# Dense products with u in three float32r terms, u split one key ahead, at the end of a hybrid-trunk step

## The chip, the cores and the metric

The kernel runs on one core of one Trainium2 chip. The metric is the device time of one execution in microseconds. Times from the trace are counted from the start of the span of one profiled execution. TensorE appears as PE (matmuls) and PEld (weight loads), VectorE as DVE, ScalarE as ACT, GpSimd as POOL, SyncE as SP.

## What is computed

One layer of a streaming encoder over 1152 tokens: 1024 of a prompt and 128 of eight sample streams, nine tiles of 128 tokens with 1024 features. A mixer (a gating unit and a retention branch, merged and projected) is followed by a retrieval over 16384 single-neuron experts, and a final norm. The change is in the retrieval. Cut to what matters there:

```python
def _peer_block(t, w_query, k1, k2, eu, ev):
    q = (t @ w_query).reshape(T, P_HEADS, P_DKEY)
    s1 = jnp.einsum('thd,nd->thn', q[..., :P_HALF], k1)
    s2 = jnp.einsum('thd,nd->thn', q[..., P_HALF:], k2)
    v1, i1 = lax.top_k(s1, P_TOPK)
    v2, i2 = lax.top_k(s2, P_TOPK)
    ...                       # the 16 best pairs of each of 8 heads
    experts = e1 * P_NKEYS + e2
    w = jax.nn.softmax(vals, axis=-1)
    a = jax.nn.gelu(jnp.einsum('td,thkd->thk', t, eu[experts]))
    return jnp.einsum('thk,thkd->td', w * a, ev[experts])
```

A token has 128 experts (8 heads of 16). Each has a row u and a row v of 1024 float32 features. The token's product with u goes through a gelu, is weighed, and scales v, which is summed.

## The kernel before

The trunk works through three groups of tiles (0 and 1; 2 to 5; 6 to 8). Its weights come through a stream of units of 128x1024 float32, in the order of the list `order`. In the first two groups each unit is split into two float32r parts, and a product is made of three terms (high with high, low with high, high with low: `products`). In the third group, from `PLAIN` on, units are used as plain float32, and the buffers of the parts (`wraw`, `whi`, `wlo`, three each) all serve as unit buffers, nine in number. `room` says when a buffer of this ring may be loaded again: when the unit in it has been taken.

The retrieval is done in two ways. Tiles 0, 1, 2, 6, 7 and 8 are gathered: for each of a token's 128 experts GpSimd issues an indirect DMA that fetches u and v side by side for 128 tokens, a row buffer of 128x2048 float32 (line 865). VectorE makes the dot with the token (`dot`, line 818, two records: the product and a read of its accumulator), ScalarE the gelu and the weight (`weigh`, 823 and 824), VectorE adds the scaled v to the sum (`add`, 828). 768 such row buffers are worked off, one after the other. The ring of buffers is a list: five called `gat`; two called `st` once the dense tiles are expanded; and one called `gax`, added just ahead of the dense loop. `AHEAD` is how many gathers stand ahead of their dots in program order.

Tiles 3, 4 and 5 are dense: a table of the weights of all 128 x 128 experts is written to DRAM (`pdr`), and the dense loop (line 1030 on) goes over 128 keys, 128 experts each. For key e, TensorE multiplies u (eight blocks of 128x128, stationary) with the transposed tokens `tT` (384 columns) into a PSUM tile S (line 1040); ScalarE makes the gelu g (1042); VectorE multiplies g with the table's part pt (1044); and two keys later (`LEAD`) TensorE adds six products of g with v into six PSUM tiles `res` (1053). S has two buffers, g four, pt one per eight keys. `turn_dense` makes `tT` during the third group's queries.

The order of instructions on each engine is set when the program is built: the loops issue keys at high priority (`DP`) and rows at a pace (`PACE`, in us of an estimated clock that `advance` moves), and the scheduler orders all by what it estimates to be ready. Each engine then follows its own order. A row's dot that waits for its landing holds back everything behind it on VectorE.

Of the kernel before, what the change touches and what calls it, by code (L numbers as in the profile page):

```python
# [8 lines left out]
F32 = mybir.dt.float32  # L9
F32R = mybir.dt.float32r  # L10
# [7 lines left out]
P = 128  # L18
# [38 lines left out]
def step_kernel(ctx: ExitStack, tc: tile.TileContext, x, state, wall, wst, bs, rows, vec, cst, smp, cosd, sind, euv,  # L57
# [51 lines left out]

    for e in range(NKEYS + LEAD):  # L110
        order += [("u", e)] * (e < NKEYS) + [("v", e - LEAD)] * (e >= LEAD)
    NRAW, NPART, NBK = 3, 3, 2
# [23 lines left out]

    def room(n, now):
        ring = rings[homes[n % 3]]
        return ring[-NPART] < now

# [143 lines left out]
    def turn_dense(pl):  # L284

        tT = hTs["dense"] = pair_tiles(act, TD, "h", gi=PLAIN)
        for n, t in enumerate(DENSE):
            xt = pl.tile([P, D], F32, name="dx", bufs=2)
            nc.sync.dma_start(xt, tsp[t])
            yield  # L290
            for j in range(2):
                ps = sp.tile([P, 4, P], F32, name="sps")
                for k in range(4):
                    tr(ps[:, k], xt[:, (4 * j + k) * P:(4 * j + k + 1) * P], ident)
                split([w[:, 4 * j:4 * j + 4, n * P:(n + 1) * P] for w in tT], ps)
# [709 lines left out]

    tT, = hTs.pop("dense")
    while len(expanded) < len(DENSE):
# [5 lines left out]
    dg = ctx.enter_context(tc.tile_pool(name="dg", bufs=1))  # L1013
    gx = ctx.enter_context(tc.tile_pool(name="gx", bufs=1))
    dp = dense_sb.enter_context(tc.tile_pool(name="dp", bufs=1))
    dps = ctx.enter_context(tc.tile_pool(name="dps", bufs=1, space=bass.MemoryType.PSUM))
    rings_.append((gx, "gax", 1))
    AHEAD[0] += 1

# [4 lines left out]
    res = {o: dps.tile([P, 512], F32, name=f"res{o[0]}{o[1]}") for o in outs}  # L1024
    G = {}

    PACE[0] = 3.55
    for e in range(NKEYS + LEAD):
        if e < NKEYS:
            with tc.high_priority(DP):  # L1030
# [4 lines left out]
                ps = Ss.pop(e) if e in Ss else dps.tile([P, TD], F32, name="S", bufs=2)  # L1035
                u, (w,) = take()
                assert u == ("u", e)
                w = w.rearrange("p a b -> p (a b)")
                for k in range(KD):
                    mm(ps, w[:, k * P:(k + 1) * P], tT[:, k], start=k == 0, stop=k == KD - 1)  # L1040
                a = G[e] = dg.tile([P, TD], F32, name="g", bufs=4)
                nc.scalar.activation(a, ps, AF.Gelu_apprx_tanh)  # L1042
# [108 lines left out]
```

## Time and profile before

| | us |
|---|---|
| median of three runs | 3848.13 |
| lowest, highest | 3837.57, 3850.18 |
| the profiled execution | 3852.71 |
| its span | 3850.9 |
| TensorE busy in the span | 3569.9 (93%) |
| VectorE busy | 3088.8 (80%) |
| ScalarE busy | 1359.1 (35%) |
| GpSimd busy | 1097.9 (29%) |

The shares are means over the trunk and the dense loop. The dense loop starts at about 2390 us. What limits each part of it is read from the stretches, where the copies of the lists of expert rows (`idx`, line 802) for tiles 7 and 8 serve as marks that both programs have.

### The profile page before, as it was taken

The numbers are of one execution on the slowest core, as the hardware profiler recorded it, in microseconds if no ns is written. First come the engines' busy times: TensorE is split into PE (matmuls) and PEld (weight loads), VectorE is DVE, ScalarE is ACT, GpSimd is POOL, SyncE is SP. The second block draws the span as 40 slices with busy tenths as digits, with TensorE's granted clock in tenths as the row PEclk, the third lists the DMA queues.
The fourth block names the chain that finished last, engine by engine and source line by source line (L and its number), as shares of the span: only waits on it lengthen the run. The fifth ranks groups of instructions, "written<-read, shape, count | busy, mean of one in ns | idle before, by whom it ended". The sixth has DMA issues, their size and how long they took to land.

```text
span 3850.9 us, 45654 instructions
## 1 busy us (share of the span) xinstructions
PE 3569.9 (93%) x15681; PEld 2468.7 (64%) x15681; DVE 3088.8 (80%) x5859; ACT 1359.1 (35%) x3289; POOL 1097.9 (29%) x788
## 2 busy tenths in 40 slices
PE   8999999999989888989999989988999899999998
PEld 6789987877878776767667565544444454444444
DVE  5666699999989789999993679979877877777773
ACT  4455634444343532846545222211112111211111
POOL 0000002433434231132320332334433534443330
PEclk9999999999999999999999989999999999999999
DMA  8675547998989895799994998899999999999993
GB/s 313 238 259 189 195 152 285 363 352 328 359 321 375 340 372 214 246 344 316 365 346 146 369 410 338 337 411 374 418 419 418 419 418 419 419 418 419 418 419 153
DMA packets 300822, 1291.28 MB, mean 335 GB/s; under 512 B 28336, under 2 KB 92592, under 8 KB 200240
## 3 DMA queue, kind: packets, MB, share of 16 engines
q0 software_dynamic: 114944, 822.13, 53.6%
q1 hardware_dynamic: 185648, 466.25, 32.9%
q8 instruction: 124, 2.03, 0.2%
q14 instruction: 106, 0.87, 0.1%
HBM read 1221.16 MB, written 67.11 MB: 335 GB/s over the span
## 4 chain that ended last, share of the span: by engine, by line
DMA 26%; issue 22%; DVE 19%; PE 19%; POOL 11%; ACT 2%; SPq 0%; POOLq 0%; DVEq 0%; ACTq 0%
DMA gat<-in_euv_dram,idx 12%; POOL gat L865 9%; PE gps L210 9%; DMA st<-in_euv_dram,idx 8%; DVE acc L828 5%; PE gps L226 4%; DVE gat L818 3%; PE res L1053 2%; PE S L1040 2%; DMA s<-ssp 1%; DMA gax<-in_euv_dram,idx 1%; POOL st L865 1%; DVE ktmp L710 1%; DVE wlo L240 1%; DVE oh L794 1%
## 5 line engine op out<-in xcount | busy, mean ns | idle before, releaser
L865 POOL DMA_INDIRECT gat<-in_euv_dram,idx x600 | 848.3, 1414 | 1905.0 <-DVE acc L828 1158.3
L828 DVE SCALAR_TENSOR_TENSOR acc<-gat,sdot,acc 128x1024 f32<-128x1024 f32 x600 | 767.0, 1278 | 106.8 <-ACT sdot L824 103.3
L818 DVE CUSTOM_DVE_ANT_0 gat<-gat,tx 128x1024 f32<-128x1024 f32 x600 | 730.1, 1218 | 134.9 <-DMA gat<-in_euv_dram,idx 117.4
L823 ACT ACTIVATE sdot<-sdot 128x1 f32<-128x1 f32 x768 | 154.9, 203 | 1788.3 <-DVE sdot L818 1787.0
L226 PE MATMUL gps<-whi,h 128*128 128x256 f32 x2688 | 519.2, 301 | 6.9 <-ACT h L236 5.7
L226 PEld LDWEIGHTS gps<-whi,h 128*128 128x128 f32 x2688 | 437.7, 193 | 28.2 <-issue 10.1
L226 PE MATMUL gps<-wlo,h 128*128 128x256 f32 x1536 | 419.6, 312 | 8.8 <-issue 5.5
L210 PE MATMUL gps<-h,whi 128*128 128x256 f32 (+2 forms) x1520 | 407.4, 366 | 4.6 <-ACT th L591 3.2
L210 PE MATMUL gps<-y,whi 128*128 128x256 f32 (+2 forms) x1168 | 310.7, 362 | 9.4 <-DVE pb L382 4.8
L226 PEld LDWEIGHTS gps<-wlo,h 128*128 128x128 f32 x1536 | 295.9, 194 | 26.9 <-issue 13.0
L210 PEld LDWEIGHTS gps<-h,whi 128*128 128x128 f32 x1520 | 270.7, 193 | 62.3 <-ACT th L591 3.8
L210 PE MATMUL gps<-h,wlo 128*128 128x256 f32 (+2 forms) x864 | 292.8, 378 | 6.6 <-DVE wlo L240 6.4
L1040 PE MATMUL S<-h,wlo 128*128 128x384 f32 x672 | 252.3, 509 | 41.6 <-ACT g L1042 41.6
L1040 PE MATMUL S<-h,wraw 128*128 128x384 f32 x688 | 258.6, 510 | 29.0 <-ACT g L1042 28.4
L865 POOL DMA_INDIRECT st<-in_euv_dram,idx x118 | 164.7, 1396 | 370.5 <-DVE acc L828 229.4
L1040 PE MATMUL S<-h,whi 128*128 128x384 f32 x688 | 248.7, 493 | 21.7 <-ACT g L1042 21.6
L1053 PE MATMUL res<-wraw,g 128*128 128x512 f32 x516 | 243.1, 594 | 1.7 <-DVE g L1044 1.7
L1053 PE MATMUL res<-wlo,g 128*128 128x512 f32 x516 | 243.7, 592 | 0.5 <-DVE g L1044 0.5
L1040 PEld LDWEIGHTS S<-h,wlo 128*128 128x128 f32 x672 | 132.7, 200 | 170.0 <-issue 65.0
L1053 PE MATMUL res<-whi,g 128*128 128x512 f32 x504 | 240.1, 595 | 0.9 <-DVE g L1044 0.9
L210 PEld LDWEIGHTS gps<-y,whi 128*128 128x128 f32 x1168 | 206.4, 192 | 51.9 <-issue 7.4
L1040 PEld LDWEIGHTS S<-h,wraw 128*128 128x128 f32 x688 | 135.8, 199 | 158.5 <-issue 67.6
(230 smaller groups left out, 5686.7 us busy)
## 6 DMA issues: line engine op xcount, KB each, us to landing
wraw<-in_wall_dram SPq DMA_DIRECT2D x214, 512.0 KB
gat<-in_wall_dram SPq DMA_DIRECT2D x84, 512.0 KB
pdr<-st SPq DMA_DIRECT2D x24, 1024.0 KB
pt<-pdr SPq DMA_DIRECT2D x16, 1536.0 KB
wlo<-in_wall_dram SPq DMA_DIRECT2D x43, 512.0 KB
whi<-in_wall_dram SPq DMA_DIRECT2D x43, 512.0 KB
wraw<-in_eud_dram SPq DMA_DIRECT2D x43, 512.0 KB
whi<-in_eud_dram SPq DMA_DIRECT2D x43, 512.0 KB
```

The costliest lines, as they stand in the source:

```text
L210: mm(ps[:, c, :T], x, y, start=kh == 0 and k == 0 and j == 0, stop=kh == nk - 1 and k == 3 and j == len(pr) - 1)
L226: mm(ps[:, i], y, x, start=kh == 0 and k == 0 and j == 0 and i % 2 == 0, stop=kh == 1 and k == 3 and j == len(pr) - 1 and last)
L240: nc.vector.tensor_tensor(parts[1], src, parts[0].bitcast(F32), op=OP.subtract)
L710: nc.vector.match_replace(tmp, v[:, :8], src, -3.0e38)
L794: tt(oh, ij[:, c, hs, None].to_broadcast([P, n, TOPK]), iota[:, None, :].to_broadcast([P, n, TOPK]), op=OP.is_equal)
L818: nc.vector.tensor_tensor_reduce(out=b[:, :D], in0=b[:, :D], in1=d["x"], op0=OP.mult, op1=OP.add, scale=1.0, scalar=0.0, accum_out=d["s"][ ...
L823: nc.scalar.activation(d["s"][:, j:j + 1], d["s"][:, j:j + 1], AF.Gelu_apprx_tanh)
L828: nc.vector.scalar_tensor_tensor(d["acc"], b[:, D:], d["s"][:, j:j + 1], d["acc"], op0=OP.mult, op1=OP.add)
L865: nc.gpsimd.indirect_dma_start(out=b, out_offset=None, in_=euv, in_offset=bass.IndirectOffsetOnAxis(ap=d["idx"][:, j:j + 1], axis=0))
L1040: mm(ps, w[:, k * P:(k + 1) * P], tT[:, k], start=k == 0, stop=k == KD - 1)
L1053: mm(res[n, j], g[:, n * P:(n + 1) * P], w[:, 512 * j:512 * j + 512], start=e == LEAD, stop=e == NKEYS + LEAD - 1)
```

## The change

The dense products with u become three-term products. `turn_dense` makes `tT` in two float32r parts. A new function `halves` takes the next u and splits it: ScalarE copies it into `uhi` (float32r), VectorE subtracts to get `ulo`; both have two buffers. It is called once ahead of key 0, and then at key e for key e+1, behind the products of key e. A key's eight float32 products become 24 of float32r. So that u can be taken one key earlier, the list `order` puts v one place later, and `room` counts a unit of u as released at once by the split. The row buffer `gax` goes, and `AHEAD` stays one lower; g has three buffers instead of four.

```diff
-    for e in range(NKEYS + LEAD):
-        order += [("u", e)] * (e < NKEYS) + [("v", e - LEAD)] * (e >= LEAD)
+    for e in range(NKEYS + LEAD + 1):
+        order += [("u", e)] * (e < NKEYS) + [("v", e - LEAD - 1)] * (e > LEAD)
...
     def room(n, now):
         ring = rings[homes[n % 3]]
-        return ring[-NPART] < now
+        return ring[-NPART] < now - (type(order[ring[-NPART]]) is tuple and order[ring[-NPART]][0] == "u")
...
-        tT = hTs["dense"] = pair_tiles(act, TD, "h", gi=PLAIN)
+        tT = hTs["dense"] = pair_tiles(act, TD, "h")
...
-    gx = ctx.enter_context(tc.tile_pool(name="gx", bufs=1))
...
-    rings_.append((gx, "gax", 1))
-    AHEAD[0] += 1
...
+    us = []
+    def halves():
+        u, (w,) = take()
+        assert u[0] == "u"
+        w = w.rearrange("p a b -> p (a b)")
+        hi = dg.tile([P, D], F32R, name="uhi", bufs=2)
+        nc.scalar.copy(hi, w)
+        lo = dg.tile([P, D], F32R, name="ulo", bufs=2)
+        nc.vector.tensor_tensor(lo, w, hi.bitcast(F32), op=OP.subtract)
+        us.append((hi, lo))
...
-                u, (w,) = take()
-                assert u == ("u", e)
-                w = w.rearrange("p a b -> p (a b)")
+                if not e:
+                    halves()
+                w = us.pop(0)
                 for k in range(KD):
-                    mm(ps, w[:, k * P:(k + 1) * P], tT[:, k], start=k == 0, stop=k == KD - 1)
-                a = G[e] = dg.tile([P, TD], F32, name="g", bufs=4)
+                    pr = products([t[:, k * P:(k + 1) * P] for t in w], [t[:, k] for t in tT])
+                    for j, (x, y) in enumerate(pr):
+                        mm(ps, x, y, start=k == 0 and j == 0, stop=k == KD - 1 and j == 2)
+                if e + 1 < NKEYS:
+                    halves()
+                a = G[e] = dg.tile([P, TD], F32, name="g", bufs=3)
```

The scheduler orders the whole end anew. In the rows below, line 818 before is 820 after (dot), 828 is 830 (add), 1044 is 1059 (product with pt), 1040 is 1053 (product with u), 1053 is 1068 (product with v), 1067 is 1082 (a dense tile's sum), and 1035 is the new subtraction.

VectorE in the long stretch, before, from one key's product with pt to the next:

```order
L1044 TENSOR_TENSOR g<-g,pt 128x384
L828 SCALAR_TENSOR_TENSOR acc<-st,sdot,acc 128x1024
L818 ISA st,sdot<-st,tx 128x1024
L818 ISA sdot 128x1
L828 SCALAR_TENSOR_TENSOR acc<-st,sdot,acc 128x1024
L818 ISA gax,sdot<-gax,tx 128x1024
L818 ISA sdot 128x1
L828 SCALAR_TENSOR_TENSOR acc<-gax,sdot,acc 128x1024
L818 ISA gat,sdot<-gat,tx 128x1024
L818 ISA sdot 128x1
L1044 TENSOR_TENSOR g<-g,pt 128x384
```

The same place after:

```order
L1059 TENSOR_TENSOR g<-g,pt 128x384
L1035 TENSOR_TENSOR ulo<-whi,uhi 128x1024
L820 ISA gat,sdot<-gat,tx 128x1024
L820 ISA sdot 128x1
L830 SCALAR_TENSOR_TENSOR acc<-gat,sdot,acc 128x1024 x2
L820 ISA st,sdot<-st,tx 128x1024
L820 ISA sdot 128x1
L830 SCALAR_TENSOR_TENSOR acc<-st,sdot,acc 128x1024
L820 ISA st,sdot<-st,tx 128x1024
L820 ISA sdot 128x1
L1059 TENSOR_TENSOR g<-g,pt 128x384
```

The subtraction for the key two ahead stands behind the product with pt, and the dot ahead of that product has its add four instructions later instead of at once.

TensorE in the long stretch, before (S is the product with u, res the six sums with v; the numbers are buffers):

```order
L1040 MATMUL S_20831<-h0_18720,whi_20670 128x384 x5
L1053 MATMUL res00_19458<-wlo_20695,g_20762 128x512
L1040 MATMUL S_20831<-h0_18720,whi_20670 128x384
L1053 MATMUL res10_19459<-wlo_20695,g_20762 128x512
L1040 MATMUL S_20831<-h0_18720,whi_20670 128x384
L1053 MATMUL res20_19460<-wlo_20695,g_20762 128x512
L1040 MATMUL S_20831<-h0_18720,whi_20670 128x384
L1053 MATMUL res01_19461<-wlo_20695,g_20762 128x512
```

TensorE after:

```order
L1053 MATMUL S_22455<-h0_18720,uhi_22424 128x384
L1053 MATMUL S_22395<-h0_18720,uhi_22364 128x384
L1053 MATMUL S_22455<-h0_18720,ulo_22426 128x384
L1053 MATMUL S_22395<-h0_18720,ulo_22366 128x384
L1053 MATMUL S_22455<-h1_18721,uhi_22424 128x384
L1053 MATMUL S_22395<-h1_18721,uhi_22364 128x384
L1053 MATMUL S_22455<-h0_18720,uhi_22424 128x384
L1053 MATMUL S_22395<-h0_18720,uhi_22364 128x384
L1053 MATMUL S_22455<-h0_18720,ulo_22426 128x384
L1053 MATMUL S_22395<-h0_18720,ulo_22366 128x384
L1068 MATMUL res00_19462<-whi_22300,g_22368 128x512
L1053 MATMUL S_22455<-h1_18721,uhi_22424 128x384
```

The products of one key are now often mixed with those of the next, and with single float32 products with v.

VectorE at the end, before: the last row's dot and add, the last six keys' products with pt, and the dense tiles' sums.

```order
L818 ISA gat,sdot<-gat,tx 128x1024
L818 ISA sdot 128x1
L828 SCALAR_TENSOR_TENSOR acc<-gat,sdot,acc 128x1024
L1044 TENSOR_TENSOR g<-g,pt 128x384 x6
L1067 TENSOR_TENSOR dx<-dx,res_19458 128x512
L1067 TENSOR_TENSOR dx<-dx,res_19459 128x512
```

VectorE after, around the last key's product with pt:

```order
L1059 TENSOR_TENSOR g<-g,pt 128x384
L830 SCALAR_TENSOR_TENSOR acc<-st,sdot,acc 128x1024
L820 ISA st,sdot<-st,tx 128x1024
L820 ISA sdot 128x1
L830 SCALAR_TENSOR_TENSOR acc<-st,sdot,acc 128x1024
L1082 TENSOR_TENSOR dx<-dx,res_19462 128x512
L1082 TENSOR_TENSOR dx<-dx,res_19465 128x512
L820 ISA gat,sdot<-gat,tx 128x1024
L820 ISA sdot 128x1
```

Behind the last key's product there are now 24 dots and 25 adds of rows, and the dense sums stand among them.

## Rows read from the trace of the kernel before

**Rows 1.** The page's 40 slices: busy share of DMA in tenths, and GB/s.

```profile
DMA  8675547998989895799994998899999999999993
GB/s 313 238 259 189 195 152 285 363 352 328 359 321 375 340 372 214 246 344 316 365 346 146 369 410 338 337 411 374 418 419 418 419 418 419 419 418 419 418 419 153
```

**Rows 2.** Stretches: length; PE, PEld, DVE, ACT, POOL busy (x); clock, DMA share, GB/s.

```profile
2434.00:2486.00 52.00, 52.00 (x143) 26.87 (x142) 50.29 (x138) 13.63 (x33) 20.59 (x16) 1.00 1.00 397
2486.00:2897.00 411.00, 373.26 (x977) 188.55 (x975) 341.26 (x620) 70.83 (x268) 175.24 (x118) 0.96 1.00 406
2897.00:3785.00 888.00, 830.84 (x2182) 421.94 (x2182) 674.36 (x858) 168.20 (x607) 337.76 (x250) 0.97 1.01 414
...
3768.00:3851.00 83.00, 70.28 (x187) 35.04 (x185) 26.88 (x37) 12.74 (x32) 0.00 (x0) 0.95 0.30 110
```

**Rows 3.** Timeline of DVE: start, duration; the lists for tiles 7 and 8.

```profile
2485.91 0.22 DVE L802 CAST idx<-m 128x128 int32<-128x128 f32 x1
...
2896.85 0.22 DVE L802 CAST idx<-m 128x128 int32<-128x128 f32 x1
```

**Rows 4.** The chain that ended last, in the dense loop: start, duration, what.

```profile
3746.00 4.51 PE S L1040 x14
3750.51 4.29 PE res L1053 x10
3756.31 4.51 PE S L1040 x14
```

**Rows 5.** Timeline of PE in the trunk: three-term products, 512 and 256 columns.

```profile
302.12 0.28 PE L210 MATMUL gps<-y,wlo 128*128 128x256 f32 x1
...
302.46 0.28 PE L210 MATMUL gps<-y,wlo 128*128 128x256 f32 x1
...
700.35 0.39 PE L210 MATMUL gps<-y,wlo 128*128 128x512 f32 x1
...
701.04 0.39 PE L210 MATMUL gps<-y,wlo 128*128 128x512 f32 x1
```

**Rows 6.** Timeline of PE: a float32r matmul (L226) between float32 ones (L469).

```profile
586.40 1.02 PE L469 MATMUL sps<-v,kt 128*128 128x512 f32 x2
586.86 0.68 PE L226 MATMUL gps<-wlo,h 128*128 128x256 f32 x1
587.38 1.02 PE L469 MATMUL sps<-v,kt 128*128 128x512 f32 x2
```

**Rows 7.** The trunk's split, by line: duration ns min/median/max, first and last start, form.

```profile
L240 DVE TENSOR_TENSOR wlo<-wraw,whi x172: 1160/1217/1236, 21.9 to 1400.4; 128x1024 fp32r<-128x1024 f32 x172
...
L234 ACT CAST whi<-wraw x172: 1027/1047/1100, 16.8 to 1397.9; 128x1024 fp32r<-128x1024 f32 x172
```

**Rows 8.** Timeline of DVE, rows already landed: dot, its add, the next dot.

```profile
3779.41 1.22 DVE L818 CUSTOM_DVE_ANT_0 gax<-gax,tx 128x1024 f32<-128x1024 f32 x1
...
3781.24 1.28 DVE L828 SCALAR_TENSOR_TENSOR acc<-gax,sdot,acc 128x1024 f32<-128x1024 f32 x1 [0.60 <-ACT sdot L824]
3782.44 1.22 DVE L818 CUSTOM_DVE_ANT_0 gat<-gat,tx 128x1024 f32<-128x1024 f32 x1
```

**Rows 9.** Waits of DVE from 2897 to 3785 us: total us, times, longest.

```profile
DVE acc L828 <- ACT sdot L824: 118.9, 199, 0.6
...
DVE g L1044 <- ACT g L1042: 6.8, 10, 1.0
```

**Rows 10.** The same from 2486 to 2897 us.

```profile
DVE acc L828 <- ACT sdot L824: 24.3, 41, 0.6
DVE v L708 <- DMA s<-ssp: 22.9, 6, 4.5
DVE gat L818 <- DMA gat<-in_euv_dram,idx: 12.9, 16, 1.4
```

**Rows 11.** Timeline of ACT at the end: the norm of the last tile.

```profile
3844.06 1.06 ACT L932 ACTIVATE ab<-acc 128x1024 f32<-128x1024 f32 x1
```

**Rows 12.** Work on gat in a stretch of the trunk: DVE, ACT, POOL busy (x).

```profile
1600.00:1700.00 100.00, 62.28 (x52) 0.00 (x0) 37.99 (x26) 1.00 1.02 378
```

More of the change, by code (lines that the diff above doesn't have):

```diff
@@ L1003, in step_kernel @@
         ready.update(GROUPS[gi])
-    tT, = hTs.pop("dense")
+    tT = hTs.pop("dense")
     while len(expanded) < len(DENSE):
```

## The prediction

> **What bounds the kernel now.** I read the page's 40 slices first, then busy time by stretch, then what VectorE waited for in each stretch, and last the durations of single instructions. The change touches only what comes after about 2390 us, so the reader should look there. In eleven of the last twelve slices the DMA engines move 418 or 419 GB/s at a busy share of 9 or more; the last one has 153 [rows 1]. No slice exceeds 419 GB/s, so I take that as the ceiling.
>
> The end has four stretches [rows 2, 3]. Until 2486 us (the copy of the list of expert rows for tile 7) VectorE is busy 50.3 of 52 us: VectorE is the bound. From 2486 to 2897 us (the same copy for tile 8) VectorE is at 341 of 411 and the DMA engines are full. From 2897 to 3785 us, where the gathered tiles end, DMA is full, TensorE at 831 and VectorE at 674 of 888. From 3785 us only the dense products are left: in 3768 to 3851 us DMA is at 0.30 and TensorE works alone. So dense keys are left over when the rows are done, at 10.31 us each: eight products with u at 4.51 us per 14 records (0.322 each, 16 per key) and six with v at 0.43 per record [rows 4].
>
> **Sizes.** A gathered row set ("row" below) is 128x2048 float32, 1.049 MB. A key brings u and v, 1.049 MB, and an eighth of pt, 0.197 MB: 1.245 MB. The order gives 117 rows and 34 keys for 2486 to 2897 us: 165.0 MB, 394 us at 419 GB/s, 17 less than the 411 taken. For 2897 to 3785 us it gives 257 rows and 80 keys: 369.1 MB, 881 us of 888. So these stretches lose 17 and 7 us against a full DMA. The durations are from one execution of 3852.7 us with a span of 3850.9, so 1.8 us lie outside the span; it is 4.6 us above the median of the three runs, 3848.1.
>
> **TensorE.** Per key 16 records of 0.322 us (5.15 us) give way to 24 of one pass. In the trunk's three-term products the record with wlo, one in three, comes every 0.69 us with 512 columns and every 0.34 with 256 [rows 5], 0.230 and 0.113 per matmul; between them 384 columns are 0.17: 24 x 0.17 = 4.1 us. The key falls from 10.31 to 9.25 us. The new order alternates float32r and float32 matmuls about ten times per key. In the trunk such an alternation cost between nothing and 0.12 us per return trip: two float32 records and one float32r one of 256 columns took 0.98 us from 586.40 to 587.38 [rows 6], exactly 2 x 0.43 + 0.12. I take 0.06, five times: 9.55 us, and keep 9.25 and 9.9 as ends. The Trainium skill, page TensorE: Matmul & The Clock Gate, section Back-to-back issue gap, gives about 131 ns per matmul of 512 columns in a stream with weight loads. This trace does not agree: 0.230 us. By the page (81 ns at 128 columns, estimate 115 ns at 384) the 24 would take 2.8 us; the sum below would be the same, since TensorE ends no stretch by either figure.
>
> **VectorE and ScalarE.** Each key adds a subtraction over 128x1024 on VectorE, 1.22 us (the same form wlo<-wraw,whi), and a copy on ScalarE, 1.05 us [rows 7]. Consecutive VectorE instructions overlap by 0.08 us [rows 8], so a subtraction costs 1.14 us, a row's dot 1.15, its add 1.20, a product with pt 0.48. ScalarE is busy 168 of 888 us; its 126 further copies (133 us over the whole end) lie beside other work, and the copy for key e+2 starts when the gelu of key e is done, while VectorE still works on rows. Against the added work stands one gain: an add that follows its own dot waits 0.60 us for ScalarE [rows 8]. The trace counts 199 such waits, 119 us, after 2897 us and 41 before it [rows 9, 10]; by the new order adds directly behind their dots number 70 and none, because other work falls between.
>
> **DMA.** Bytes are the same, but two things move. The row ring goes from eight buffers to seven. And the order changes its mix: when the list for tile 7 is copied, 9 keys are done (10 before); at the list for tile 8, 49 (44 before); and when the last key's product is made 744 of 768 rows have been dotted, where all were before. The surplus at the end is now rows, not keys. Loads of u and v are still released four keys or more ahead (nine unit buffers, u freed by the split instead of the matmuls), so I cost the SP queue at nothing; if that cover failed, a missed key would cost about what VectorE's longest wait for a small load costs now, 4.5 us [rows 10].
>
> **The sum.**
> Until the list for tile 7, VectorE sets the end. By then the new order has 11 subtractions (12.5 us) and six more over 512 columns for the second part of h (half of 1.22, 3.7 us), and it is behind by three adds, two dots and one product (6.4 us): 2486 + 10 = 2496 us. Ends +5 and +16.
>
> To the list for tile 8, 117 rows and 40 keys: 172.5 MB, 412 us. VectorE needs 341 + 40 x 1.14 + 6 x 0.48 = 390 us, and none of the 24 us for adds. With the same loss as now, 17 us: 430 us. Ends 412 and 443 (VectorE's 390 with today's 23 and 13 us of waits for landings [rows 10], and 17).
>
> To the last product, 235 rows and 79 keys: 344.8 MB, 823 us. VectorE: 674 less 22 rows at 2.35 and five products, plus 77 subtractions (88 us) and 70 x 0.6: 752 us. TensorE: 79 x 9.55 = 754 us (730 to 782), now 814. Both have a tenth of slack or less and hand over to each other each key, so I take 20 us of loss where 7 are now: 843 us. Ends 828 (823 and 5 of loss) and 890 (the ring's rival below, at a trip of 26.5 us: 843 + 1.4 x 34).
>
> The last 24 rows: 24 dots, 25 adds, 16 waits of 0.6 give 67 us; the dense tiles' sums and norms on VectorE, 8 us, and a wait for the last products, 4 us: 79 us. DMA needs 60 for 24 rows, so VectorE's chain of 3.02 us per row [rows 8] decides. Ends 67 and 92 (3.85 us per row, as 26 of them took in 100 us of the trunk [rows 12]). Behind the last add stands the norm of the last tile, from its square at 3844.06 to the end of the span: 7 us [rows 11].
>
> 2496 + 430 + 843 + 79 + 7 = 3855 us of span, 3857 of time, and 4.6 less in terms of the median: 3852 us, no change. TensorE's saving, 0.76 us x 128 = 97 us, is real, but it is off the path while DMA is full, and what it frees at the end (66 us of dense keys) is filled by 24 rows at 3.02 us plus 22 us of added VectorE and ring losses.
>
> **The rivals.**
> *Faster: DMA stays as full as now.* For it: VectorE's need after 2897 us falls from 800 of 888 (91%) to 752 of 843 (89%). Against: TensorE is as close. With 2491, 422, 830, 74 and 7 the span ends at 3824, in terms of the median 3821 us (-0.7%). Chance 0.33.
>
> *Slower: the row's trip does not shrink with the ring.* The trip of a buffer (issue, landing, dot, add, issue) is now 8 x 888 / 257 = 27.6 us. Seven buffers give the 843 us only if it falls to 7 x 843 / 235 = 25.1; from there each further us costs 235 / 7 = 34 us. For it: between a dot and its add the new order puts other work, which holds the buffer two to four us longer. Against: with five buffers the trunk issued 26 rows in 100 us [rows 12], a trip of 19 us with DMA also full. At 26.1 us the time is 3886; at the full 27.6, 3937. Chance 0.20.
>
> *Slower: weight loads pace the single passes.* If an alternating float32r matmul cannot go below 0.24 us, a key is 24 x 0.24 + 5.16 = 10.9 us and TensorE becomes the bound: at the granted 0.97 of 2897 to 3785 us, 79 keys take 888 us, and the 40 before take 450: 3917 us. Against: 0.113 us with 256 columns, where weights also change each time. Chance 0.08.
>
> *Slower: the clock.* In 2486 to 2897 us TensorE was busy 373 of 411 us and its granted clock was 0.96; with 52 of 52 it was 1.00 [rows 2]. The mean lies between 1.2 and 2.4 GHz, so parts ran at 1.2. With more idle time it could fall further: at 0.88 a key is 10.9 us, and the time is as in the rival before, about 3917 us. The same page, section What's actually happening, says that an idle TensorE falls to 1.2 GHz; the trace agrees in direction. Against: TensorE stays above 88% busy by the sum. Chance 0.04.
>
> *The change doesn't do what it says:* TensorE gains nothing because order, not rate, sets it. Then 3852 us is still the forecast, since TensorE ends no stretch; it is inside it.
>
> **How the numbers follow.** Forecast 0.35, faster 0.33, slower 0.20 + 0.08 + 0.04 = 0.32. About 0.3%, 11.5 us, is what a measurement of this kernel can tell from no change, so same is 3836.6 to 3859.6. Range: the floors (2491, 412, 828, 67, 7) give 3805 of span, 3802 in terms of the median, and DMA loses something everywhere, so the low end is 3808; the ring at 26.5 us gives 3900, and the full price of the two TensorE rivals and the rest of the ring's lie above it, with less than 0.15 together. The range is 3808 to 3900; the forecast's own, 3838 to 3866.
>
> **What would show it.** Right: S records of about 0.17 us spacing; VectorE at some 85% of the long stretch; DMA near 415 GB/s to the last key; about 24 rows after it, 3 us apart, with TensorE idle. Wrong: DMA well under 410 GB/s with rows waited for (the ring), TensorE over 97% busy (weight loads or clock), or fewer than ten rows left at the last product. The weakest term is the 20 us of loss: it decides the sign.

## The result, and the profile after

Against 3846.87 us (median of seven runs of the kernel before) the changed kernel takes 3816.88 us, median of seven. The ratio is 0.9931, with a 95% interval from 0.9916 to 0.9947: 0.7% faster. Beside the later experiments it was measured once more, at 0.9942 (0.9920 to 0.9963). The forecast was 3852 us, no change, with 3838 to 3866 as its own range. The time lies near that of the faster rival (3821 us).

The profiled execution took 3823.18 us, with a span of 3821.4. From its page, the 40 slices (busy share of DMA in tenths, GB/s), to be read beside [rows 1]:

```profile
DMA  8665537998989996788994899799999999999996
GB/s 310 237 254 200 198 131 287 356 370 336 358 330 370 352 375 224 246 339 302 366 350 159 348 412 367 288 418 417 417 418 382 418 419 418 418 409 418 418 413 269
```

From the 27th slice on DMA runs at 417 to 419 GB/s but for three slices (382, 409 and 413), and the last slice holds 269 where it held 153. The copies of the lists for tiles 7 and 8 on the timeline of VectorE (they answer to [rows 3]):

```profile
2483.08 0.22 DVE L804 CAST idx<-m 128x128 int32<-128x128 f32 x1
...
2899.62 0.22 DVE L804 CAST idx<-m 128x128 int32<-128x128 f32 x1
```

And the stretches between these marks, the last key's product (ends at 3728.9 us) and the end of the span; columns as in [rows 2]. The first begins at the last `x<-x,gps` of the trunk (2260.1 us here, 2267.6 before); the fifth row is the whole from there:

```profile
2260.10:2483.08 222.98, 186.11 (x717) 125.03 (x715) 209.65 (x631) 65.34 (x161) 59.57 (x41) 0.92 0.86 339
2483.08:2899.62 416.54, 387.74 (x1436) 263.50 (x1434) 383.85 (x665) 112.46 (x316) 188.48 (x118) 0.97 1.02 416
2899.62:3728.90 829.28, 765.59 (x2825) 518.84 (x2823) 699.07 (x872) 232.70 (x639) 340.22 (x236) 0.97 1.01 413
3728.90:3821.40 92.50, 5.42 (x12) 2.20 (x12) 67.94 (x87) 21.38 (x64) 30.49 (x19) 0.55 0.68 266
2260.10:3821.40 1561.30, 1344.86 (x4985) 909.57 (x4983) 1360.50 (x2251) 431.88 (x1179) 618.76 (x412) 0.94 0.97 395
```

The kernel before, cut at the same places (the third row ends where its rows are done, since keys were left over there):

```profile
2267.60:2485.91 218.31, 202.76 (x662) 118.31 (x661) 200.53 (x621) 58.13 (x158) 65.78 (x44) 0.97 0.87 344
2485.91:2896.85 410.94, 373.20 (x977) 188.63 (x975) 341.20 (x619) 70.83 (x268) 175.24 (x118) 0.96 1.00 406
2896.85:3785.50 888.65, 831.49 (x2183) 422.19 (x2183) 675.01 (x860) 168.20 (x607) 337.76 (x250) 0.97 1.01 414
3785.50:3850.90 65.40, 52.78 (x139) 26.03 (x137) 12.95 (x21) 8.72 (x17) 0.00 (x0) 0.93 0.24 87
2267.60:3850.90 1583.30, 1460.23 (x3958) 755.16 (x3956) 1229.69 (x2117) 305.88 (x1050) 578.78 (x412) 0.97 0.95 389
```

The trunk ended 7.5 us earlier in one execution than in the other. Over all kernels below that place lies between 2243 and 2268 us, and in two profiled executions of the changed kernel itself it lies 12 us apart, so it scatters by a good part of what the change is worth. Lengths from this trunk mark on are what can be compared between single profiles, where the same kernel repeats within 3 us: 1583.3 before, 1561.3 after, 22 us less. Whether any of the other 8 of the 30 us between the medians belongs to the change, these profiles can't tell.

**An account of DMA.** 1583.3 us at 389 GB/s are 616 MB; 1561.3 us at 395 are 617 MB. The bytes from the trunk mark to the end are the same, so the kernels differ only in the time in which DMA was not full. For each stretch I take its length x (1 - GB/s / 419). This is bookkeeping: with the same bytes, the length less the lost time is the bytes over 419 GB/s whatever limits the kernel. It shows where time went, and not what kept DMA from moving more. (A rate is rounded to 1 GB/s, which is 2 us in the third stretch.) Before: 218.3 x 75/419 = 39.1 to the first list, 12.7 to the second, 10.6 to the last row, 51.8 for the dense keys behind it: 114 us. After: 42.6, 3.0, 11.9 and 33.8: 91 us. That is 23 us less, and the span from the mark shrank by 22. Of it 18 us lie in the fourth stretch, where 66 us in which only TensorE worked became 92 us in which 25 rows are still worked off; 10 us lie in the second; the first and third took 5 back.

### The profile page after: what moved, and what is told of

It is laid out like the page before. It is cut to its first block, busy times and chain, and to the rows that moved or that the text cites. A ratio compares the mean times of both kernels' runs of the same rounds, so it can differ in the third digit from the quotient of the medians.

```text
span 3821.4 us, 47842 instructions
## 1 busy us (share of the span) xinstructions
PE 3450.3 (90%) x16705; PEld 2621.5 (69%) x16705; DVE 3220.5 (84%) x5993; ACT 1486.0 (39%) x3418; POOL 1143.2 (30%) x788
## 4 chain that ended last, share of the span: by engine, by line
issue 25%; DVE 24%; DMA 19%; PE 17%; POOL 11%; ACT 3%; SPq 0%; POOLq 0%; DVEq 0%; ACTq 0%
DMA gat<-in_euv_dram,idx 12%; POOL gat L867 10%; PE gps L212 8%; DVE acc L830 7%; PE gps L228 4%; DVE gat L820 3%; DMA st<-in_euv_dram,idx 2%; DMA s<-ssp 1%; DVE ulo L1035 1%; POOL st L867 1%; PE S L1053 1%; DVE ktmp L712 1%; DVE wlo L242 1%; DVE st L820 1%; DVE oh L796 1%
## 5 line engine op out<-in xcount | busy, mean ns | idle before, releaser
L867 POOL DMA_INDIRECT gat<-in_euv_dram,idx x636 | 936.9, 1473 | 2008.0 <-DVE acc L830 1179.1
L820 DVE CUSTOM_DVE_ANT_0 gat<-gat,tx 128x1024 f32<-128x1024 f32 x636 | 774.5, 1219 | 131.1 <-DMA gat<-in_euv_dram,idx 109.4
L830 DVE SCALAR_TENSOR_TENSOR acc<-gat,sdot,acc 128x1024 f32<-128x1024 f32 x636 | 813.5, 1279 | 52.6 <-ACT sdot L826 47.1
L1053 PE MATMUL S<-h,uhi 128*128 128x384 f32 x2048 | 713.3, 434 | 46.8 <-ACT uhi L1033 45.2
L1053 PEld LDWEIGHTS S<-h,uhi 128*128 128x128 f32 x2048 | 386.9, 195 | 231.7 <-issue 171.6
L1053 PE MATMUL S<-h,ulo 128*128 128x384 f32 x1024 | 407.7, 438 | 66.2 <-DVE ulo L1035 65.7
L1053 PEld LDWEIGHTS S<-h,ulo 128*128 128x128 f32 x1024 | 195.0, 195 | 169.0 <-DVE ulo L1035 89.6
L867 POOL DMA_INDIRECT st<-in_euv_dram,idx x132 | 193.8, 1468 | 388.3 <-DVE acc L830 233.3
L1068 PE MATMUL res<-whi,g 128*128 128x512 f32 x516 | 259.6, 594 | 0.7 <-DVE g L1059 0.7
L236 ACT CAST whi<-wraw 128x1024 fp32r<-128x1024 f32 x172 | 179.9, 1046 | 156.5 <-PE gps L212 89.3
```

What stands on the lines that cost most here:

```text
L236: nc.scalar.copy(parts[0], src)
L820: nc.vector.tensor_tensor_reduce(out=b[:, :D], in0=b[:, :D], in1=d["x"], op0=OP.mult, op1=OP.add, scale=1.0, scalar=0.0, accum_out=d["s"][ ...
L830: nc.vector.scalar_tensor_tensor(d["acc"], b[:, D:], d["s"][:, j:j + 1], d["acc"], op0=OP.mult, op1=OP.add)
L867: nc.gpsimd.indirect_dma_start(out=b, out_offset=None, in_=euv, in_offset=bass.IndirectOffsetOnAxis(ap=d["idx"][:, j:j + 1], axis=0))
L1053: mm(ps, x, y, start=k == 0 and j == 0, stop=k == KD - 1 and j == 2)
L1068: mm(res[n, j], g[:, n * P:(n + 1) * P], w[:, 512 * j:512 * j + 512], start=e == LEAD, stop=e == NKEYS + LEAD - 1)
```

## The experiments

Every kernel was compared with the kernel before on the same chip. The bytes are the same in all of them: the length from the trunk mark, less the time lost to DMA, is 1470 us within 2 us in each of the rows below. So the last column says no more than the second, and the ones between say where. "Lost" is worked out as above; the third stretch ends with the rows or the keys, whichever is done first.

| kernel | ratio to before (95%) | from trunk mark | lost: to list 7 | to list 8 | to end of rows or keys | behind | lost in all |
|---|---|---|---|---|---|---|---|
| before | 1 | 1583.3 | 39 | 13 | 11 | 52 | 114 |
| changed | 0.9931 (0.9916 to 0.9947) | 1561.3 | 43 | 3 | 12 | 34 | 91 |
| changed, again | 0.9942 (0.9920 to 0.9963) | 1561.8 | 44 | 3 | 10 | 34 | 90 |
| b_ring7 | 0.9973 (0.9961 to 0.9984) | 1575.4 | 32 | 9 | 13 | 52 | 105 |
| a_fp32u | 1.0067 (1.0049 to 1.0085) | 1611.4 | 49 | 23 | 21 | 48 | 142 |
| a_one | 0.9975 (0.9962 to 0.9988) | 1578.4 | 49 | 17 | 19 | 23 | 108 |
| a_one_ring8 | 0.9949 (0.9932 to 0.9965) | 1569.4 | 52 | 6 | 26 | 16 | 99 |
| a_nolo | 0.9917 (0.9898 to 0.9936) | 1554.4 | 37 | 10 | 6 | 32 | 85 |
| a_two | 1.0016 (1.0005 to 1.0027) | 1595.7 | 42 | 9 | 9 | 65 | 124 |
| a_dx | 0.9918 (0.9902 to 0.9934) | 1558.9 | 43 | 4 | 12 | 29 | 87 |
| a_dx2 | 0.9916 (0.9900 to 0.9932) | 1561.8 | 43 | 5 | 14 | 30 | 91 |
| a_dx_early | 1.0002 (0.9993 to 1.0012) | 1585.8 | 46 | 30 | 10 | 30 | 116 |
| a_one_ring8_dx_early | 1.0043 (1.0028 to 1.0059) | 1609.3 | 56 | 44 | 24 | 15 | 139 |

**The buffer alone.** b_ring7 is the kernel before without `gax`:

```diff
-    gx = ctx.enter_context(tc.tile_pool(name="gx", bufs=1))
...
-    rings_.append((gx, "gax", 1))
-    AHEAD[0] += 1
```

> The kernel before without the row buffer gax: seven row buffers, AHEAD one lower, nothing else. Theory A (the end is limited by the DMA engines' 419 GB/s and then by the dense keys that are left over; a row's trip shrinks with the ring): no change, 3847 us within 0.3%, DMA still 418 GB/s from 2900 us on. Rival R (the trip through a buffer stays 27.6 us, so one buffer less is one eighth fewer rows in flight): the 888 us stretch grows by 34 us for each us by which the trip stays above 24.2, so 3890 us or more, with VectorE waiting for landings and DMA clearly under 410 GB/s.

Measured: 3831.98 us against 3842.19, ratio 0.9973. Its stretches to list 7, to list 8 and to the last row:

```profile
2250.60:2460.81 210.21, 196.60 (x646) 115.64 (x645) 196.63 (x618) 57.58 (x156) 62.66 (x42) 0.97 0.89 356
2460.81:2870.75 409.94, 383.53 (x998) 193.66 (x996) 345.89 (x624) 71.60 (x271) 169.23 (x120) 0.97 1.00 410
2870.75:3760.20 889.45, 829.09 (x2182) 420.31 (x2182) 676.23 (x860) 168.56 (x607) 326.65 (x251) 0.98 1.01 413
```

The long stretch takes 889.4 us, 888.7 before: with seven buffers in place of eight the trip of a row shrank by an eighth, and rival R falls. "No change within 0.3%" holds by its number only: seven buffers are 0.3% faster, and the interval leaves 1 out. Most of the gain stands in the first row, 210.2 us for 218.3. In the traces 391 rows instead of 393 are added ahead of the list for tile 7, and two rows at 2.35 us of VectorE would be 4.7 of these 8 us; this was not tried by itself.

**Without the rate.** a_fp32u:

```diff
-        tT = hTs["dense"] = pair_tiles(act, TD, "h")
+        tT = hTs["dense"] = pair_tiles(act, TD, "h", gi=PLAIN)
...
-        us.append((hi, lo))
+        us.append((w,))
...
-                        mm(ps, x, y, start=k == 0 and j == 0, stop=k == KD - 1 and j == 2)
+                        mm(ps, x, y, start=k == 0 and j == 0, stop=k == KD - 1 and j == len(pr) - 1)
```

> The changed kernel with everything but the rate: u is still copied and split one key ahead, but the parts are not read, and the products with u are float32 again (16 records of 0.322 us per key). Theory A (what the change gives is TensorE's rate: keys get done under the cover of the DMA): the gain is gone. Dense keys are left over when the rows are done, as before, and the split's VectorE work shows in the stretch before 2486 us: 3850 to 3862 us. Rival B (the gain is the order: rows instead of keys at the end, u taken a key earlier, seven buffers): 3817 to 3825 us.

Measured: 3868.30 us, ratio 1.0067, beyond even theory A's range; rival B's time is missed by more. VectorE's waits from 2920 to 3760 us, the largest, and the stretch behind the last row:

```profile
DVE ulo L1035 <- ACT uhi L1033: 70.2, 22, 8.0
```

```profile
3807.40:3867.00 59.60, 46.91 (x123) 22.93 (x121) 12.43 (x19) 8.72 (x17) 0.00 (x0) 0.93 0.22 79
```

Dense keys are left over again (60 us with DMA at 79 GB/s), and DMA loses 23 and 21 us where b_ring7 lost 9 and 13. But this run takes away more than the rate. Its products read u in the unit buffer, so the buffer is held until they are done, where the changed kernel gives it back with the split. What the queue that loads units (line 162) and ScalarE waited for from 2920 to 3720 us, in a_fp32u:

```profile
SPq L162 <- PE S L1053: 393.8, 59, 16.9
ACT uhi L1033 <- DMA whi<-in_eud_dram: 33.4, 7, 7.3
ACT uhi L1033 <- DMA wraw<-in_eud_dram: 33.4, 7, 10.1
ACT uhi L1033 <- DMA wlo<-in_eud_dram: 26.6, 7, 7.8
```

and in the changed kernel, where ScalarE waits for no load:

```profile
SPq L162 <- DVE ulo L1035: 276.5, 67, 11.1
```

So the copies came late because u landed late (93 us of waits), and VectorE waited for the copies (70 us). The steps are: the buffer -10 us (3842.2 to 3832.0); the split and the new order, with u's buffers held longer and one buffer of `g` less, +36 (to 3868.3); the rate and the early release of u's buffers together -50 (to 3818.8, the changed kernel in its second measurement, beside 3843.9 us of the kernel before). How the 50 divide is not shown, since no run took the rate back alone.

**Rows and keys ending together.** a_one has one buffer each for `uhi` and `ulo`; a_one_ring8 has that and `gax` back (eight row buffers):

```diff
-        hi = dg.tile([P, D], F32R, name="uhi", bufs=2)
+        hi = dg.tile([P, D], F32R, name="uhi", bufs=1)
...
-        lo = dg.tile([P, D], F32R, name="ulo", bufs=2)
+        lo = dg.tile([P, D], F32R, name="ulo", bufs=1)
```

> The changed kernel with one buffer each for uhi and ulo instead of two. By the program's order 766 of 768 rows are then added when the product of key 126 is made, where the changed kernel has 737: almost no rows are left over behind the last key. Theory A (DMA full up to the last key, and the 84 us tail of the changed kernel, 57 us of them worth of DMA, is lost time): from 2483 us 542.5 MB at 419 GB/s are 1295 us, with 11 us of loss and some 20 for sums and norm 3809 of span, less if the sums lie beside rows: 3795 to 3808 us. Rival S (with one buffer the split of the next key waits for this key's last product, and TensorE then waits for copy, subtraction and what stands before it on VectorE, more than the 5.2 us of products with v can hide): a key takes over 11 us, 119 keys 1309 us or more, 3820 to 3870 us, with long waits of PE for ulo.

> The same single buffers for uhi and ulo, and the 8 KB per partition that they free go back to the eighth row buffer gax (AHEAD one higher). Theory A (the ring's size is worth nothing while DMA is full): as a_one within 0.3%. Rival R (one more row in flight counts): faster than a_one by 10 us or more. Rival S as for a_one: over 3820 us.

Measured: 3834.50 (0.9975) and 3819.86 us (0.9949). The tail did shrink, to 23 and 16 us lost, but theory A's 3795 to 3808 was missed by both. What PE waited for from 2490 to 3720 us, in a_one:

```profile
PE S L1053 <- DVE ulo L1035: 111.0, 78, 7.3
PE S L1053 <- ACT uhi L1033: 26.2, 22, 4.2
```

and in the changed kernel:

```profile
PE S L1053 <- DVE ulo L1035: 64.7, 40, 7.3
PE S L1053 <- ACT uhi L1033: 23.6, 13, 4.8
```

TensorE waits 137 us for the split instead of 88: rival S, within its 3820 to 3870 us for a_one. a_one_ring8 waits nearly as long (102.7 and 27.8 us) and is 15 us faster, as rival R had it; theory A's "as a_one within 0.3%" falls, and rival S's 3820 us is just missed. But by the account the two differ by 11 us ahead of list 8 alone (17 against 6 lost), mostly in one dip of a_one:

```profile
2640.00:2680.00 40.00, 32.78 (x117) 23.72 (x116) 30.30 (x55) 8.46 (x24) 15.20 (x10) 0.87 0.85 311
```

That is 10 us lost in 40, at about the place where the kernel before also has one (below), and the two orders differ (527 and 522 rows added at key 50). Whether the buffer or the order takes the dip away is open.

**Slack of the engines.** a_nolo takes the subtraction from VectorE; a_two takes a third of the products with u from TensorE; the changed kernel ran beside them.

```diff
-        lo = dg.tile([P, D], F32R, name="ulo", bufs=2)
-        nc.vector.tensor_tensor(lo, w, hi.bitcast(F32), op=OP.subtract)
-        us.append((hi, lo))
+        us.append((hi, hi))
```

```diff
-                    for j, (x, y) in enumerate(pr):
-                        mm(ps, x, y, start=k == 0 and j == 0, stop=k == KD - 1 and j == 2)
+                    for j, (x, y) in enumerate(pr[:2]):
+                        mm(ps, x, y, start=k == 0 and j == 0, stop=k == KD - 1 and j == 1)
```

> The changed kernel once more, unchanged, to stand beside the next three on one chip: 0.993 of the kernel before within 0.2%, about 3816 us.

> The changed kernel without VectorE's part of the split: the subtraction is left out, and the 24 matmuls of a key read uhi where they read ulo (so the products with u are not the reference's). VectorE is relieved of 128 x 1.14 = 146 us, and by the order 19 rows instead of 25 are left at the last key. Theory A (DMA is full up to the last key, so the added VectorE work costs only where VectorE is the bound: nine keys ahead of the mark at 2483 us, 10 us, and nothing in the 1246 us after it; the tail has six rows less, of which the DMA time is paid anyway): 3800 to 3808 us, and DMA at 413 to 417 GB/s as in the changed kernel. Rival V (the subtraction delays rows all along): 3780 us or less, with DMA nearer to 419 GB/s from 2490 us on.

> The changed kernel with two of the three terms (the product of the high part of u with the low part of h is left out, so the output is less exact): 16 matmuls per key instead of 24, which takes another 8 x 0.173 x 128 = 177 us from TensorE. By the order 87 rows instead of 25 are left at the last key. Theory A (TensorE's rate is worth nothing once the keys end under the cover of the DMA; what is saved comes back as rows in the tail, which VectorE works off at 3.02 us each): 2483 + 444.2 MB at 419 GB/s (1060) + 11 + 87 x 3.02 + 27 + 8 = 3852 us, or 3806 us if the tail runs at the DMA's 2.5 us per row. Rival T (TensorE's rate is still the bound behind 2483 us): under 3790 us.

Measured: 3818.82, 3811.51 (0.9917) and 3850.35 us (1.0016). a_nolo from list 8 to its last key's product:

```profile
2888.39:3735.30 846.91, 782.07 (x2890) 532.53 (x2888) 631.75 (x808) 233.48 (x650) 314.82 (x239) 0.97 1.02 416
```

VectorE is at 632 of 847 us (75%) instead of 699 of 829 (84%), and from list 7 to the last product 16 us are lost (10 + 6) where the changed kernel lost 15 (3 + 12). The gain is 7 us in the medians, with intervals that overlap (theory A: 11 to 19, rival V: over 35; neither is met). In the profiles it lies ahead of list 7, as theory A had it: 212.9 us instead of 224.7 and 223.0.

a_two, from list 8 to the last product and behind it:

```profile
2963.76:3566.50 602.74, 544.26 (x1793) 335.78 (x1791) 501.36 (x624) 168.25 (x461) 249.69 (x165) 0.95 1.01 413
3566.50:3846.90 280.40, 5.56 (x13) 2.28 (x12) 218.60 (x273) 56.96 (x192) 132.24 (x81) 0.52 0.88 322
```

177 us of TensorE's work are gone and the kernel is 0.7% slower than the changed one. The keys are done at 3566 us, and 87 rows follow, which VectorE works off in 272 us (3.13 us per row), with DMA at 322 GB/s to the end. Theory A's 3852 us held within 2, in part by luck: list 7 came 10 us later than in its sum, and the tail was 18 us shorter. Rival T falls for this order. The order itself puts the 87 rows last, and `PACE`, which sets how rows are spread among keys, was not moved with it; so what a faster TensorE is worth with rows and keys ending together was not measured.

**The tail.** In the changed kernel's tail VectorE waited for the residual of the dense tiles, and GpSimd in turn for buffers. These are rows of its timeline from 3736 to 3752 us:

```profile
3736.28 1.29 DVE L1082 TENSOR_TENSOR dx<-dx,res 128x512 f32<-128x512 f32 x2 [2.99 <-DMA dx<-xsp]
...
3743.84 1.88 DVE L1082 TENSOR_TENSOR dx<-dx,res 128x512 f32<-128x512 f32 x3 [5.14 <-DMA dx<-xsp]
...
3751.51 2.88 POOL L867 DMA_INDIRECT gat<-in_euv_dram,idx  x1 [17.01 <-DVE acc L830]
```

a_dx fetches it at key 124, into a buffer of `pt` that is free by then, and the norm's row and scratch take the place of the other `pt`:

```diff
+                if e == NKEYS - 4:
+                    xb = pp[0].tile([P, TD // LT, BE, LT], F32, name="pt").rearrange("p c e t -> p (c e t)")
+                    xts = [xb[:, n * D:(n + 1) * D] for n in range(len(DENSE))]
+                    for n, t in enumerate(DENSE):
+                        nc.sync.dma_start(xts[n], xsp[t])
...
```

> The changed kernel, with the dense tiles' residual (dx) fetched at key 124 into a buffer of pt that is free by then, and the norm's row and scratch in the other one, instead of all after the last key. In the tail VectorE waited 2.99 and 5.14 us for dx, and from 3733 to 3751 us no gather was issued. Theory A (the tail is a chain of VectorE, so a wait that goes there is worth its length, and the DMA engines have less to make up): 8 to 15 us faster than a_again, 3801 to 3809 us. Rival (the tail is set by what DMA still has to bring, 24 rows x 2.5 us): within 3 us of a_again.

> a_dx once more, to stand beside the next two on one chip: 0.992 of the kernel before within 0.2%, about 3812 us.

Measured: 3812.06 us (0.9918), and 3813.38 (0.9916) on another chip, so some 6 us faster than the changed kernel in the medians; the intervals overlap, and from the trunk mark the profiles show 1558.9 and 1561.8 us against 1561.3 and 1561.8. Theory A's 8 to 15 us and the rival's 3 are both missed. From the last product to the end:

```profile
3726.40:3811.10 84.70, 5.42 (x12) 2.20 (x12) 68.03 (x87) 23.47 (x66) 29.45 (x19) 0.56 0.71 276
```

The tail is 84.7 us instead of 92.5, so 8 us shorter, the length of the waits that went. But the stretch ahead of it is 832.7 us (834.6 in a_dx2) instead of 829.3 (828.1): the three tiles, 1.57 MB, are now fetched where DMA is full, and 1.57 MB at 419 GB/s are 3.8 us. I had not counted that. It has the lowest time of the kernels that make the true three terms, but a gain over the changed kernel is not shown beyond the noise.

**Starting the rows of tile 7 earlier.** a_dx_early is a_dx with another priority for the choice of experts; a_one_ring8_dx_early has this, the early `dx` and the buffers of a_one_ring8.

```diff
-    BOOST = [100]
+    BOOST = [1000]
```

> a_dx with the choice of experts (top-k and lists) at higher priority than the dense loop's work (BOOST 1000 instead of 100). By the order the list for tile 7 is copied on VectorE after 6 keys and 386 adds instead of 9 and 390: three keys (1.62 us each on VectorE) and four rows (2.35) less stand ahead of it, 14 us. Theory A (ahead of that mark VectorE is the bound and DMA stands partly idle, behind it DMA is full, so work moved across it is hidden, and rows start earlier): 7 to 14 us faster than a_dx, 3798 to 3805 us, with the mark some 10 us or more earlier and DMA as full as before behind it. Rival (the three keys and four rows moved behind the mark lengthen what comes after it by as much): within 3 us of a_dx2.

> a_one_ring8 (single uhi and ulo, eight row buffers; the order ends rows and keys together) with dx fetched early and the higher priority for the choice of experts; by the order 5 keys and 388 adds stand ahead of the list for tile 7 (9 and 393 in a_one_ring8). Theory A (DMA sets the end; the tail behind the last row was 26 us with dx waits of 5.9 us): 3800 us within 6, at least as fast as a_dx_early. Rival S (a TensorE that waits for the single-buffered split of the next key becomes the bound as soon as DMA starts earlier): 3812 us or more, with over 80 us of waits of PE for ulo.

Measured: 3845.55 (1.0002) and 3861.63 us (1.0043): a_dx_early is 32 us slower than a_dx2, where 7 to 14 faster was expected (the rival: within 3). The mark did come earlier, and then (a_dx_early, to list 7, to list 8, and a piece in which they meet):

```profile
2258.60:2468.21 209.61, 162.57 (x620) 107.84 (x618) 195.53 (x624) 61.01 (x151) 52.35 (x37) 0.91 0.84 327
2468.21:2936.03 467.82, 436.65 (x1614) 299.99 (x1615) 411.80 (x684) 121.06 (x334) 181.87 (x124) 0.96 0.97 392
```

```profile
2450.00:2540.00 90.00, 72.90 (x260) 49.54 (x259) 85.56 (x290) 20.23 (x47) 20.05 (x13) 0.91 0.78 294
```

The higher priority pulled the choice of experts for tile 8 forward as well. VectorE was busy for 86 of these 90 us, with the small instructions of that choice between the rows, GpSimd issued 13 gathers where the changed kernel issued 25, and DMA fell to 294 GB/s (417 in the changed kernel): 90 x 125/419 = 27 us lost, nearly the whole difference. My expectation had looked at one mark only. a_one_ring8_dx_early lost 44 us to list 8 in the same way. Its time lies in rival S's range, but TensorE waited for the split no longer than in a_one_ring8 (102.1 and 29.1 us), so that isn't its cause.

## Why the prediction was wrong

The sum was made against the profiled execution of before. Counted from the trunk mark, 2267.6 us, it forecast 1587.4 us, and 1561.3 were measured:

| stretch | predicted | measured |
|---|---|---|
| trunk mark to list 7 | 228.4 | 223.0 |
| to list 8 | 430 | 416.5 |
| to the last key's product | 843 | 829.3 |
| the rows left over | 79 | 84.4 |
| to the end of the span | 7 | 8.1 |

**The two losses** are the step that failed: together 27 us too much, where the whole sum is 26 too long. The sign hung on them. The prediction called the second of them its weakest term. The other terms cancel, 5 us too long to list 7 and 6 too short behind the last key. The faster rival had the losses at 10 and 7 us, for DMA that "stays as full as now"; its stretches (223, 422, 830, 74 and 7 us) come to 1556, and that this lies within 5 us of the measured 1561 is in part luck, since its second is 5 too long and its fourth 10 too short.

To list 8 I charged "the same loss as now, 17 us". The changed kernel lost 4.5 by the same count of rows and keys at 419 GB/s (416.5 less 412), 3.0 by the rate. In the trace of before the loss (13 us by the rate) sits nearly whole in 120 us, 2560 to 2680, at a mean of 377 GB/s (12 us lost), with its bottom at 343; b_ring7 has such a dip too, at 340, and the changed kernel is full at the same place. One row each, of before, b_ring7 and the changed kernel:

```profile
2600.00:2640.00 40.00, 26.19 (x61) 13.10 (x61) 33.48 (x93) 6.00 (x23) 17.77 (x10) 0.83 0.93 343
```

```profile
2560.00:2600.00 40.00, 33.71 (x80) 16.79 (x79) 34.34 (x91) 6.11 (x23) 18.84 (x11) 0.89 0.91 340
```

```profile
2600.00:2640.00 40.00, 39.12 (x151) 26.56 (x151) 38.80 (x72) 11.11 (x31) 21.25 (x14) 1.00 1.02 418
```

An event at one place does not belong to a stretch as a share, and I should have sliced the stretch to see where its 17 us lay. It goes with VectorE's waits for the scores (22.9 us before [rows 10], of which 18.4 in these 120 us; 12.2 after). But the waits alone don't make it: a_fp32u has 12.1 us of them and loses 23, a_dx_early 4.1 and loses 30. It also goes with how densely the order packs the choice of experts for tile 8: its first steps (MAX8, line 708, 710 after) lie within 121 us before, 112 in b_ring7 and 118 in a_nolo, which all dip, and within 227 in the changed kernel; but a_one spreads them over 229 us and dips. What takes the dip away was not tried, so this part of the gain belongs to the order and its cause stays open.

To the last product I charged 20 us for both engines being within a tenth of full, where the kernel before loses 7 by count (10.6 by the rate). The changed kernel lost 6 by the same count (829.3 less 823), 11.9 by the rate. There was no row for the 20. Over half of the 11.9 is again one event, 6.7 us in the first 80 us behind list 8, where a dot waits 9.1 us for a tile's tokens (`tx`). Behind it the changed kernel, a_nolo (146 us less on VectorE) and a_two (177 less on TensorE) all run at 416 GB/s. The changed kernel in two pieces, then the others behind their first 80 us:

```profile
2899.62:2980.00 80.38, 68.14 (x244) 46.45 (x243) 64.84 (x88) 26.95 (x66) 34.05 (x22) 0.92 0.95 384
2980.00:3728.90 748.90, 697.45 (x2583) 472.39 (x2581) 634.23 (x785) 205.75 (x574) 306.16 (x214) 0.97 1.01 416
```

```profile
2970.00:3735.30 765.30, 707.84 (x2613) 482.67 (x2613) 574.26 (x730) 208.07 (x587) 287.14 (x218) 0.97 1.01 416
3044.00:3566.50 522.50, 475.39 (x1568) 293.49 (x1566) 435.77 (x540) 146.26 (x399) 215.55 (x143) 0.95 1.02 416
```

So more slack of either engine gained nothing there, and little slack costs at most the 5 us that are lost in 749. Losses of 19 to 26 us do stand in this stretch of a_fp32u, a_one, a_one_ring8 and a_one_ring8_dx_early, but TensorE's busy share isn't what sets them apart (832 of 896 us in a_fp32u, 766 of 829 in the changed kernel). These are the kernels in which copies waited for u, or TensorE waited longest for the split; which of that costs what was not tried.

**To list 7**: 5 us more than before, not 10; the lower end. Against b_ring7, which has nearly the same rows ahead of the mark (391 adds, 390 here), it is 12.8 us more, where the sum had 16 for the added work. The row of before shows TensorE at 52 of 52 us there as well [rows 2]; that VectorE is the bound is borne out for the changed kernel by a_nolo, whose mark comes 10 to 12 us sooner.

**TensorE.** Spacing of S as forecast. Timeline of PE in the changed kernel, first a run of single passes, then S between float32 pairs:

```profile
3712.49 0.51 PE L1053 MATMUL S<-h,uhi 128*128 128x384 f32 x2
3712.84 0.33 PE L1053 MATMUL S<-h,ulo 128*128 128x384 f32 x1
3713.01 0.51 PE L1053 MATMUL S<-h,uhi 128*128 128x384 f32 x2
...
3720.42 1.02 PE L1068 MATMUL res<-wlo,g 128*128 128x512 f32 x2
3720.88 0.74 PE L1053 MATMUL S<-h,uhi 128*128 128x384 f32 x1
3721.45 1.02 PE L1068 MATMUL res<-wlo,g 128*128 128x512 f32 x2
```

Three matmuls in 0.52 us are 0.173 each. The sustained spacing of the Trainium skill (TensorE: Matmul & The Clock Gate, Back-to-back issue gap), by which I had estimated 0.115 us, is not borne out here. Between two float32 pairs 1.03 us pass, and 2 x 0.43 + 0.173 is 1.03: the alternation costs nothing in these rows. The prediction took 0.06 for it from [rows 6], where the 0.12 us beyond two records is the float32r matmul itself (0.113 with 256 columns). A key is then 24 x 0.173 + 12 x 0.43 = 9.3 us, not 9.55; it changed nothing, as the sum said.

**The rows left over**: 24 dots and 25 adds, as the order had it. In the second half they stand 3.03 us apart, as the prediction had it, each add 0.60 us behind its dot; timeline of VectorE in the changed kernel:

```profile
3793.82 1.28 DVE L830 SCALAR_TENSOR_TENSOR acc<-gat,sdot,acc 128x1024 f32<-128x1024 f32 x1 [0.60 <-ACT sdot L826]
...
3796.85 1.28 DVE L830 SCALAR_TENSOR_TENSOR acc<-gat,sdot,acc 128x1024 f32<-128x1024 f32 x1 [0.60 <-ACT sdot L826]
```

Of the 5 us more, 4 are the waits for `dx`, 8.1 us, where I had allowed 4 for the last products; 1 is left open. In a_two 87 such rows took 3.13 us each, with the dense sums among them.

**DMA.** The ring rival fell with b_ring7 and with the trip found here, 7 x 829 / 236 = 24.6 us. The loads of u and v were rightly costed at nothing (one wait of `ulo` for a load, 0.4 us); a_fp32u shows the cover failing, with ScalarE waiting 93 us for them, up to 10.1 at a time, where I had put a missed key at 4.5. One sentence on the change is wrong: `room` does not count a unit of u as released at once, it lets its buffer be loaded one take later than before. The rivals of weight loads and clock did not show: granted 0.97, 413 GB/s.

"TensorE's saving is real, but it is off the path while DMA is full" is not shown. Behind the last row the 66 us of dense keys were on the path, and the sum knew it. But of the 50 us between a_fp32u and the changed kernel only 15 lie behind the last row or key; 6 lie ahead of list 7, 20 between the lists and 10 behind them, and there too the rate and the early release of u were worth time once the split was in. The two together are worth 50 us, the rest of the change costs 26, and the forecast had its gains and costs as equal. That the keys now end under the rows because TensorE is faster is argued from the price of a key (9.3 us instead of 10.31) and the marks; that the rate alone is enough for it was not run. VectorE's need to the last product adds up to 750 us, not 752; nothing hung on it.

## What to carry to other kernels

Where one resource is full for most of a stretch, count the time in which it is not full, by place: the count says where time is lost, and an experiment must say why. Cut a stretch into pieces before a loss is carried over, since a loss may be a single event, and charge nothing for "little slack" without a row that shows it. When a run is to take away one part of a change, look in its trace for what else it takes away: here the old rate also held u's buffers. A transfer that is moved out of an idle place into a full one costs its bytes there (3 to 6 us for 1.57 MB here).

## What was not expected of the hardware

Alternating float32r and float32 matmuls on TensorE costs nothing that these rows show (1.03 us for two float32 records of 0.43 and one float32r matmul of 0.173). One row buffer fewer did not slow a stretch in which DMA was full: 889.4 us with seven, 888.7 with eight. A full busy share of the DMA engines is not a full rate: it is 1.02 at 378 GB/s in the trunk [rows 12] and 1.02 at 418 in the dense loop.
